# Decay exponents from spare rows of a TensorE product, two-part operands for y_diag and dt, and shortened norm chains, in a two-layer trunk

## The chip, the cores and the metric

The kernel runs on one core of one Trainium2 chip. The metric is the device time of one execution in microseconds (us), and lower is better. Engines are named as in the profile: PE is TensorE (the matrix engine), PEld its loading of the stationary operand, DVE VectorE, ACT ScalarE, POOL GpSimd, SP SyncE, which issues the DMAs.

## The reference

Input x holds 512 tokens of 1024 features in float32. Layer 0 runs Mamba-2 (SSD) heads and forgetting attention behind one projection; layer 1 is a causal convolution module. Each layer is `x + RMSNorm_post(mixer(RMSNorm_pre(x)))`. The part that matters most here is the SSD, with 16 heads of 64 features in 4 groups, 4 chunks of 128 tokens and a state of 128:

```python
xd = x * dt;  da = dt * a;  cs = cumsum(da over the 128 tokens of a chunk)
seg = cs[l] - cs[s]                                    # l query, s key, one head
decay = exp(where(l >= s, seg, -inf))
cb = einsum('bclgn,bcsgn->bclsg', cc, bc)              # one per group and chunk
y_diag = einsum(cb * decay, xd)
chunk_states = einsum(bc, xd * exp(cs[-1] - cs));  h = h * exp(cs[-1]) + state
y_off = einsum(cc, h_in) * exp(cs)
y = rmsnorm_by_group((y_diag + y_off + xs * d_skip) * silu(z_ssd)) * ssd_norm
o = softmax(q k / 8 + c_t - c_s, causal) v * silu(z_fox)     # c = cumsum(log forget gate)
x = x + rmsnorm(concat(y, o) @ w_out, g_post)
```

## The kernel before

Every product is done in float32r with each operand split into a high and a low part: `hi` is a cast, `lo` a subtraction, and a product is three matmuls, hi·hi, hi·lo and lo·hi (`mm3`, three calls of `mm` at line 102, so that all matmuls of the profile have that line, and are told apart by their tiles).

The weights are cut into 138 jobs of 0.5 MB, each worked off in 8 chunks of three matmuls of 512 columns (or six of 256): jobs 0 to 55 are the in-projection of layer 0 (xbc, z_ssd, z_fox, v, q and k), 56 to 71 its output projection, 72 to 121 the in-projection of layer 1, 122 to 137 its output projection. In the code `JO` is 56, `J1` 72 and `JO1` 122. `out_proj` computes the first half of the columns in jobs 56 to 63 (`first`) and the second in 64 to 71 (`second`), and `finish(b)` does the norm of one block of 128 tokens when its last product is there.

TensorE runs in the order in which the code is written. A planner, `Steps`, puts the steps of the SSD and of attention between the chunks of the jobs: a step may start when its needs are done and a delay has passed, counted in estimated TensorE microseconds (`now`, raised by each matmul). The delays of the SSD are the twelve numbers `DL`; `DL[11]` is that between the scaling by the gated norm (`gs`) and the transposes `yT`. The other engines are ordered by a scheduler, in which `high_priority` moves work ahead, and each of them works through its queue in order.

The steps of one SSD group: `silus` and `bc_parts` make B and C and their parts; `x_tokens` transposes x and scales it by dt (`xd`, split into parts); `cbT` makes the product cb and copies it out; `seg(h)` makes the decay exponents of a head: a matmul (`bc`) whose stationary operand is a column of `sel2`, broadcast, spreads cs[l] to all 128 partitions, then four DVE operations, one per chunk, add −cs[s] (`tk`) and a mask of 0 or a large negative number (`maskT`), and ACT takes the exponent. `mprod(h)` multiplies by cb and splits; `ydiag(h)` does three matmuls of 64 columns per chunk; `states` and `state_parts` make the running state H and its parts (`hll` is a low part); `yoff` the inter-chunk part `yo`; `gate` adds yd into y and multiplies by silu(z); `gate_sums` and `gate_scale` are the group's norm.

For 52 of the later weight tiles the low part is prepared beforehand. This early stream (`lo_ahead`) loads a weight tile (`pre`, line 202), casts it on ACT (`prh`, line 211), subtracts on DVE (line 212) and stores the low part to DRAM (`lo`, line 216). `run` calls it once per so many chunks, as the diff shows.

`rstd_of` (line 346 its DVE operation, 348 the power on POOL) and `scaled` (364, 367) are the norms; line 106 is the transposes. `dt` is a product of 48 columns (`dtf`), done together with the first three jobs in two halves of 256 tokens.

Of the kernel before, what the change touches and what calls it, by code (L numbers as in the profile page):

```python
# [12 lines left out]
ALU = mybir.AluOpType  # L13
# [23 lines left out]
def trunk(  # L37
# [306 lines left out]
    def rstd_of(ss, n):  # L344
        v = col("var", ss.shape[-1])
        V.tensor_scalar(v, ss, 1.0 / n, EPS, ALU.mult, ALU.add)  # L346
# [10 lines left out]

    def scaled(dst, xs):

        s2 = col("s2", 2)  # L360
        for i, t in enumerate(xs):
            sumsq(t, s2[:, i : i + 1])
        if len(xs) == 2:
            V.tensor_tensor(s2[:, 0:1], s2[:, 0:1], s2[:, 1:2], ALU.add)
        r = rstd_of(s2[:, 0:1], D)
# [59 lines left out]
    G.memset(maskT, 0.0)  # L425
    G.affine_select(out=maskT, in_=maskT, compare_op=ALU.is_ge, fill=NEG, base=0,
# [205 lines left out]
    def out_proj(w, stages, nk, gpost, resid, done, hooks):  # L632
# [27 lines left out]
        def first(k2, wh, wl):  # L660
# [46 lines left out]
        def finish(b):  # L707
            ss = sumsq(pb1[b])
            y1 = [o0[b], t2("y1")]
            V.tensor_tensor(y1[1], pb1[b], gpost[1], ALU.mult)  # L710
            V.tensor_tensor(ss, ss, s0[b], ALU.add)
            r = rstd_of(ss, D)
# [392 lines left out]
    dh, dl = t2("dh", F32R)[:, : KT * 48], t2("dl", F32R)[:, : KT * 48]  # L1105
    wdt = [lambda k, t=t: t[:, k * 48 : (k + 1) * 48] for t in (dh, dl)]
# [15 lines left out]
    split(dh, dl, raw[:, : KT * 48], A.copy, V)  # L1122
# [69 lines left out]
    chl = cp.tile([80, 2, S], F32R, name="chl")  # L1192
# [3 lines left out]
    V.tensor_scalar(chl[64:80], f32(chl)[32:48], -1.0, None, ALU.mult)  # L1196

# [404 lines left out]
```

## Time and profile before

| what | value |
|---|---|
| time, median of 3 runs | 939.8 us (937.92 to 940.81) |
| profiled execution | 940.86 us |
| its span, first to last instruction | 939.1 us |
| granted TensorE clock, mean | 0.993 of full |
| PE busy | 906.6 us (97%) |
| DVE busy | 731.1 us (78%) |
| ACT busy | 605.3 us (64%) |
| POOL busy | 511.6 us (54%) |
| data moved | 166.14 MB, 177 GB/s over the span |

In a row of the profile, `out<-in` are the tiles written and read, then come partitions × elements and the count; "busy" is the time with at least one such instruction at work, and the "mean" is that of one from its start to its modelled end, so that the means of pipelined matmuls overlap. In a timeline each line begins with the start and the duration, and the bracket tells how long the engine stood idle before and what it waited for. In a table of windows the columns are the length, then the busy time (and count) of PE, PEld, DVE, ACT and POOL, the granted clock, the DMA share and GB/s.

### The profile page before, as it was taken

The page shows a single profiled execution, that of the slowest core. Times are in us where ns is not written, and L with a number is a line of the kernel's source. Part 1 is how long each engine was busy: PE and PEld are TensorE (multiplying, and loading weights), DVE is VectorE, ACT ScalarE, POOL GpSimd, SP SyncE. Part 2 cuts the span into 40 slices and gives each one's busy share as a digit, 9 for nine tenths or more (in the row PEclk, how much of TensorE's full clock was granted, in tenths as well). Part 3 has the DMA queues.
Part 4 walks back from the last instruction along what each step waited for, and adds up shares of the span by engine and source line. Part 5 has one row for each costly group of instructions (what it writes and reads, how often), then busy time and mean ns, then how long its engine had stood idle before and what let it go on. Part 6 is the DMA issues. An engine that isn't in the chain of part 4 may idle for free.

```text
span 939.1 us, 13909 instructions
## 1 busy us (share of the span) xinstructions
PE 906.6 (97%) x4683; PEld 755.6 (80%) x4683; DVE 731.1 (78%) x1284; ACT 605.3 (64%) x1134; POOL 511.6 (54%) x476
## 2 busy tenths in 40 slices
PE   6999999998999999989899989999999999999997
PEld 6887787787798888778678879888888887787885
DVE  5667968788977887988877347899999999979502
ACT  5757667576855767677575536987886877658300
POOL 2604554535633444445573111998999999847310
PEclk9999999999999999999999999999999999999999
DMA  7725631347765574674538986546564665554503
GB/s 208 229 77 180 202 90 53 104 128 237 241 202 159 163 243 158 182 244 150 168 110 285 333 301 227 169 157 213 180 209 150 190 197 174 157 157 155 182 1 112
DMA packets 182507, 166.14 MB, mean 177 GB/s; under 512 B 7900, under 2 KB 151908, under 8 KB 182436
## 3 DMA queue, kind: packets, MB, share of 16 engines
q1 hardware_dynamic: 182420, 165.25, 54.9%
q8 instruction: 37, 0.61, 0.3%
q14 instruction: 34, 0.28, 0.1%
q10 hardware_dynamic: 16, 0.00, 0.0%
HBM read 133.64 MB, written 31.46 MB: 176 GB/s over the span
## 4 chain that ended last, share of the span: by engine, by line
PE 42%; DVE 6%; DMA 5%; issue 2%; ACT 2%; SPq 1%; POOL 1%; DVEq 0%; POOLq 0%; ACTq 0%
PE m L102 29%; PE o L102 10%; DMA lo<-pre 3%; DVE pre L212 2%; DMA wr<-in_o_w_in_dram 1%; PE acc L102 1%; PE tm L102 1%; DMA wr<-in_e_w_out_dram 1%; DVE w L191 1%; PE s L102 1%; DVE pl L119 1%; PE pT L106 0%; DMA pre<-in_o_w_in_dram 0%; ACT pr L95 0%; DMA pre<-in_o_w_out_dram 0%
## 5 line engine op out<-in xcount | busy, mean ns | idle before, releaser
L102 PE MATMUL m<-uh,w 128*128 128x512 f32 (+1 forms) x1392 | 453.5, 393 | 0.0
L102 PEld LDWEIGHTS m<-uh,w 128*128 128x128 f32 x1392 | 261.4, 190 | 50.9 <-issue 3.1
L102 PE MATMUL m<-ul,w 128*128 128x512 f32 (+1 forms) x696 | 267.7, 385 | 0.0
L191 POOL TENSOR_TENSOR w<-wr,w 128x512 fp32r<-128x512 f32 x112 | 158.8, 1442 | 160.3 <-ACT w L159 123.6
L984 DVE SCALAR_TENSOR_TENSOR acc<-h,cw,acc 128x490 f32<-128x490 f32 (+13 forms) x274 | 179.0, 731 | 2.7 <-ACT acc L976 2.0
L891 POOL TENSOR_TENSOR acc<-acc,prod 128x507 f32<-128x507 f32 (+9 forms) x124 | 159.6, 1289 | 8.2 <-ACT prod L877 0.7
L102 PEld LDWEIGHTS m<-ul,w 128*128 128x128 f32 x696 | 132.3, 190 | 21.5 <-issue 0.5
L102 PE MATMUL o<-w,hlh 128*128 128x512 f32 x448 | 142.2, 399 | 2.3 <-ACT pr L95 2.3
L212 DVE TENSOR_TENSOR pre<-pre,prh 128x512 fp32r<-128x512 f32 x104 | 90.6, 889 | 44.8 <-ACT prh L211 44.6
L102 PEld LDWEIGHTS o<-w,hlh 128*128 128x128 f32 x448 | 83.4, 191 | 19.0 <-ACT pr L95 3.0
L102 PE MATMUL tm<-w,uh 128*128 128x256 f32 (+1 forms) x384 | 91.7, 330 | 1.9 <-ACT pr L95 0.9
L211 ACT CAST prh<-pre 128x512 fp32r<-128x512 f32 x104 | 61.2, 622 | 48.5 <-DMA pre<-in_o_w_in_dram 14.6
L1464 POOL TENSOR_SCALAR pr<-pr,ri 128x128 f32<-128x128 f32 (+1 forms) x64 | 39.7, 621 | 92.6 <-DVE ri L1463 85.8
L159 ACT CAST w<-wr 128x1024 fp32r<-128x1024 f32 x72 | 74.8, 1048 | 23.0 <-DMA wr<-in_e_w_in_dram 6.6
L102 PE MATMUL o<-w,hll 128*128 128x512 f32 x224 | 88.0, 393 | 0.0
L877 ACT ACTIVATE prod<-h,cw 128x507 f32<-128x507 f32 (+9 forms) x124 | 79.0, 709 | 0.0
L348 POOL TENSOR_TENSOR rstd<-var,mhalf 128x1 f32<-128x1 f32 (+1 forms) x20 | 14.0, 698 | 114.6 <-DVE var L346 114.6
L157 ACT CAST w<-wr 128x1024 fp32r<-128x1024 f32 x56 | 57.2, 1050 | 18.5 <-DMA wr<-in_o_w_out_dram 10.3
L102 PEld LDWEIGHTS tm<-w,uh 128*128 128x128 f32 x384 | 62.9, 190 | 7.6 <-DVE QS L605 1.1
L102 PE MATMUL tm<-w,ul 128*128 128x256 f32 (+1 forms) x192 | 61.2, 319 | 0.0
L95 ACT ACTIVATE pr<-s,nmx 128x128 f32<-128x128 f32 (+1 forms) x64 | 34.0, 531 | 38.0 <-DVE nmx L1458 27.8
L102 PEld LDWEIGHTS o<-w,hll 128*128 128x128 f32 x224 | 42.6, 190 | 9.0
(270 smaller groups left out, 1594.3 us busy)
## 6 DMA issues: line engine op xcount, KB each, us to landing
wr<-in_e_w_in_dram SPq DMA_DIRECT2D x56, 512.0 KB
lo<-pre SPq DMA_DIRECT2D x52, 512.0 KB
pre<-in_o_w_in_dram SPq DMA_DIRECT2D x48, 512.0 KB
wr<-in_o_w_in_dram SPq DMA_DIRECT2D x48, 512.0 KB
w<-lo SPq DMA_DIRECT2D x48, 512.0 KB
wr<-in_e_w_out_dram SPq DMA_DIRECT2D x16, 512.0 KB
wr<-in_o_w_out_dram SPq DMA_DIRECT2D x16, 512.0 KB
x<-in_x_dram SPq DMA_DIRECT2D x12, 256.0 KB
```

What stands on the lines that cost most here:

```text
L95: i = A.activation(*a, **kw)
L102: T.matmul(o, l, r, start=start, stop=stop, skip_group_check=True)
L157: last_cast[0] = A.copy(hi, src).ins
L159: last_cast[0] = A.copy(hi, src).ins
L191: j.eng.tensor_tensor(hl[1][i][:, sl], src[:, sl], f32(hl[0][i])[:, sl], ALU.subtract)
L211: A.copy(h[:, sl], t[:, sl])
L212: V.tensor_tensor(t.bitcast(F32R)[:, sl], t[:, sl], f32(h)[:, sl], ALU.subtract)
L348: mark["rstd"] = G.tensor_tensor(r, v, mhalf.to_broadcast([P, ss.shape[-1]]), ALU.pow).ins
L877: A.activation(prs[i][:, s:], hs[j][:, : S - s], AF.Copy, scale=w31(30 - s, j))
L891: G.tensor_tensor(a2[j][:, s:], a2[j][:, s:], prs.pop(i)[:, s:], ALU.add)
L984: V.scalar_tensor_tensor(a[:, s:], h[:, : S - s], w31(30 - s, j), a[:, s:], ALU.mult, ALU.add)
L1464: G.tensor_scalar(p[:, :L], p[:, :L], ri, 1.0, ALU.mult, ALU.mult)
```

## The change

Parts, in the order of the diff:

1. The early stream runs at one call per 7 chunks up to job 69, where it ran at one per 11 from job 56 on.
2. The norm chains: the first half's sum of squares is already scaled and given EPS by `part_var`, and `rstd_of` takes it in with the second half's. `finish` calls `rstd_of` before the product with `gpost`.
3. `z_ssd`, `v_proj` and the first job of layer 0's `out_proj` loop over token blocks outside and weight rows inside.
4. dt: the high and low part of its weights stand in one operand of 112 columns, so that two matmuls per row tile do the three products; the result's two pieces are added by one more DVE operation.
5. Exponents: the stationary operand of `bc` is a tile `sel` of 128 rows, made once per group: rows 0 to 47 choose cs of the head, and rows 64 to 71 hold cs of the keys in hi and lo for the four chunks (16 small DMAs from `chl`), against indicator rows in `cs2`. The matmul so gives cs[l] − cs[s], and one DVE operation bounds it at 88. The mask holds 1 and 0, and is multiplied into cb as it is copied out, on DVE.
6. `ydiag`: `xd` tiles hold hi and lo of a head side by side, and hi of the decay product is multiplied with both at once (128 columns), lo with hi (64 columns). `yadd` adds the pieces into y for each pair of heads, four operations; `gate` only multiplies.
7. `states` and `state_parts` get high priority on DVE and ACT; `DL[11]` goes from 6 to 9.

```diff
-                if 5 <= i < 13 or 26 <= i:
-                    if (8 * i + c) % (11 if i >= JO else 7 if i >= 26 else 8) == 0:
+                if 5 <= i < 13 or 26 <= i < J1 - 2:
+                    if (8 * i + c) % (7 if i >= 26 else 8) == 0:
                         next(early, None)
...
+    def rstd_of(ss, n, pre=None):
+            V.scalar_tensor_tensor(v, ss, 1.0 / n, pre, ALU.mult, ALU.add)
+    def part_var(ss, n):
+        p = col("pre")
+        V.tensor_scalar(p, ss, 1.0 / n, EPS, ALU.mult, ALU.add)
...
-            for j in range(2):
-                k = 2 * k2 + j
-                for b in range(NB):
+            for b in range(NB):
+                for j in range(2):
+                    k = 2 * k2 + j
...
         def finish(b):
             ss = sumsq(pb1[b])
+            r = rstd_of(ss, D, s0[b])
             y1 = [o0[b], t2("y1")]
             V.tensor_tensor(y1[1], pb1[b], gpost[1], ALU.mult)
-            V.tensor_tensor(ss, ss, s0[b], ALU.add)
-            r = rstd_of(ss, D)
...
+    def dt_chunks(sl):
+        for k in range(KT):
+            w = dhl[k // 4][:, k % 4 * P : k % 4 * P + 112]
+            mm(first[0][:112, sl], w, uh[k][:, sl], k == 0, False)
+            mm(first[0][:48, sl], w[:, :48], ul[k][:, sl], False, k == KT - 1)
...
+    cs2 = cp.tile([P, S], F32R, name="cs2")
+    V.tensor_tensor(cs2[64:72, :].rearrange("p (c l) -> p c l", c=4), i4[0], i4[1], ALU.add)
-    DL = [2, 7, 4, 11, 4, 9, 4, 9, 9, 3, 3, 6]
+    DL = [2, 7, 4, 11, 4, 9, 4, 9, 9, 3, 3, 9]
...
+        sel = st["sel"] = t2("sel", F32R)
+        G.memset(f32(sel), 0.0)
+        A.copy(h4(sel[:48, :]), f32(sel2)[:48, 4 * g : 4 * g + 4].unsqueeze(2).to_broadcast([48, 4, P]))
+        for h in range(4):
+            r = 96 + 4 * g + h
+            nc.sync.dma_start(f32(sel)[64:72, h * P : h * P + P], f32(chl)[r : r + 1, :, :])
...
-            A.copy(st["cb"], cb)
+            V.tensor_tensor(st["cb"]..., cb..., maskT.unsqueeze(1).to_broadcast([P, 4, P]), ALU.mult)
...
-        mm(bc, sel2[:, h : h + 1].to_broadcast([48, P]), cs2, True, True)
+        mm(bc, SG[h // 4]["sel"][:, h % 4 * P : h % 4 * P + P], cs2, True, True)
-        for c in range(NB):
-            V.scalar_tensor_tensor(s[:, tok(c)], bc[:, tok(c)], tk[:, c, 32 + h : 33 + h], maskT, ALU.add, ALU.add)
+            V.tensor_scalar(s, bc, 88.0, None, ALU.min)
...
-            mm3(o, mh[:, tok(c)], ml[:, tok(c)], xh, xl, True, True)
+            mm(o, mh[:, tok(c)], x, True, False)
+            mm(o[:, :64], ml[:, tok(c)], x[:, :64], False, True)
+    def yadd(g, pair):
+            for i in range(2):
+                for t in range(2):
+                    V.tensor_tensor(ys, ys, parts[:, :, :, t, :], ALU.add)
     def gate(g):
-                V.tensor_tensor(y[i], y[i], yd[i], ALU.add)
```

How it moves the instructions, at three places. On DVE at the end of layer 0, where the norm of the second block of tokens is finished (`y` is the product with `gpost`, `ss` and `var` the norm's sums, `pre` the early stream's subtraction, `u` the input of layer 1), before:

```order
L710 TENSOR_TENSOR y_1329_6195<-o_1258_5902,x_5662 128x512 [waits Activation_49]
L711 TENSOR_TENSOR ss_6192<-ss_6192,ss_5881 128x1
L212 TENSOR_TENSOR pre_6102<-pre_6102,prh_6247 128x512 [waits DMAHW7_49,DMAHW4_49,Activation_49]
L346 TENSOR_SCALAR var_6198<-ss_6192 128x1 [waits DVE_49]
L212 TENSOR_TENSOR pre_6102<-pre_6102,prh_6247 128x512 [waits Activation_49]
L714 SCALAR_TENSOR_TENSOR o_1248_5880<-o_1248_5880,rstd_6200,x_6070 128x512 [waits Pool_49]
```

and after:

```order
L349 SCALAR_TENSOR_TENSOR var_6182<-ss_6179,pre_5875 128x1 [waits DVE_49,Activation_49]
L717 TENSOR_TENSOR y_1362_6186<-o_1294_5908,x_5642 128x512
L719 SCALAR_TENSOR_TENSOR o_1278_5871<-o_1278_5871,rstd_6184,x_6074 128x512 [waits DMAHW7_49,Pool_49]
L719 SCALAR_TENSOR_TENSOR y_1362_6186<-y_1362_6186,rstd_6184,x_6075 128x512 [waits DMAHW0_49,DVE_49]
L364 TENSOR_SCALAR pre_6199<-ss_6196 128x1 [waits Activation_49]
```

The two subtractions of the early stream are gone from between the norm's operations (they stand ahead of the first block's norm now), and `var` comes before the product. (The `pre` of L364 is the norm's column, not the stream's tile.)

On PE in the first SSD group, where the exponents of its first heads stand among the z_ssd product `tm`, before:

```order
L102 MATMUL bc_960<-cs_564,sel_565 128x512 [waits DVE_49,PE_49]
L102 MATMUL tm_786<-w_793,uh_143 128x512
L102 MATMUL tm_786<-w_793,uh_143 128x512 [waits Pool_49]
L102 MATMUL tm_786<-w_793,ul_151 128x512
L102 MATMUL bc_971<-cs_564,sel_565 128x512 [waits DVE_49,PE_49]
```

and after:

```order
L102 MATMUL bc_969<-cs_561,sel_820 128x512 [waits DVE_49,DMAHW4_49,PE_49,Activation_49]
L102 MATMUL tm_786<-w_791,uh_140 128x512 x2
L102 MATMUL tm_786<-w_791,ul_148 128x512
L102 MATMUL bc_977<-cs_561,sel_820 128x512 [waits DMAHW5_49,DVE_49,PE_49]
L102 MATMUL tm_786<-w_791,uh_141 128x512 x2
```

The order of `bc` and `tm` is much the same; `bc` now waits for one of the DMAs that fill `sel`, and `tm` stays with a block of tokens (tm_786) where the block changed.

On SP at the same group (`wr` are weights of the jobs, `pre` and `lo` the early stream's load and store), before:

```order
L216 DMA lo_851<-pre_707 128x1024 [waits DMAHW2_49,DVE_49]
L163 DMA wr_1094<-in_e_w_in_dram 128x8x128 [waits DMAHW7_49,Activation_49,Pool_49]
L202 DMA pre_853<-in_o_w_in_dram 128x8x128 [waits DMAHW2_49]
L216 DMA lo_928<-pre_744 128x1024 [waits DMAHW5_49,DVE_49]
L202 DMA pre_930<-in_o_w_in_dram 128x8x128 [waits DMAHW6_49,DMAHW5_49]
```

and after:

```order
L216 DMA lo_856<-pre_705 128x1024 [waits DMAHW2_49,DVE_49]
L163 DMA wr_1091<-in_e_w_in_dram 128x8x128 [waits DMAHW7_49,Activation_49,Pool_49]
L1287 DMA sel_820<-chl 8x1x128 [waits Pool_49]
L1287 DMA sel_820<-chl 8x1x128 [waits DMAHW5_49]
L1287 DMA sel_820<-chl 8x1x128 [waits DMAHW6_49]
L1287 DMA sel_820<-chl 8x1x128
L202 DMA pre_858<-in_o_w_in_dram 128x8x128 [waits DMAHW2_49,DMAHW0_49]
```

The four small DMAs stand behind a weight load and ahead of the early stream's next load, and the first of them waits for POOL, which clears `sel`.

More of the change, by code (lines that the diff above doesn't have):

```diff
@@ L356, in sumsq @@
         return ss
+    def part_var(ss, n):
+        p = col("pre")
+        V.tensor_scalar(p, ss, 1.0 / n, EPS, ALU.mult, ALU.add)
+        return p
     def scaled(dst, xs):
[L360 to L365, printed above, removed]
+        pre = part_var(sumsq(xs[0]), D)
+        r = rstd_of(sumsq(xs[1]), D, pre)
         for t, u in zip(xs, dst):
@@ L424, in trunk @@
     maskT = cp.tile([P, P], F32, name="maskT")
-    G.memset(maskT, 0.0)
-    G.affine_select(out=maskT, in_=maskT, compare_op=ALU.is_ge, fill=NEG, base=0,
+    G.memset(maskT, 1.0)
+    G.affine_select(out=maskT, in_=maskT, compare_op=ALU.is_ge, fill=0.0, base=0,
                     pattern=[[1, P]], channel_multiplier=-1)
@@ L664, in first @@
                     lead_in()
-            for j in range(2):
-                k = 2 * k2 + j
-                for b in range(NB):
+            stagger = k2 == 0 and len(stages) == 1
+            for j, b in ((j, b) for b in range(NB) for j in range(2)) if stagger else ((j, b) for j in range(2) for b in range(NB)):
+                    k = 2 * k2 + j
                     step(pb0[b], b, k, wh(j), wl(j))
@@ L1121, in trunk @@
     to_uT(uh, ul, 0, us[0:2], c0, True)
-    split(dh, dl, raw[:, : KT * 48], A.copy, V)
+    dt_parts()
     for b in range(2, 4):
@@ L1126, in trunk @@
             split_to(b)
-    ws = [wdt] + [jobs[i].w for i in range(3)]
+    ws = [None] + [jobs[i].w for i in range(3)]
     def together(js, half):
-        gens = [fm_chunks(first[i], P if i else 48, *ws[i], uh, ul, slice(half * 256, half * 256 + 256)) for i in js]
+        sl = slice(half * 256, half * 256 + 256)
+        gens = [fm_chunks(first[i], P, *ws[i], uh, ul, sl) if i else dt_chunks(sl) for i in js]
         for _ in zip(*gens):
@@ L1202, in trunk @@
     V.tensor_copy(cs2[32:48, :], f32(csl)[0:16, :])
-    V.tensor_tensor(sel2, ident[0:48, 0:16], ident[0:48, 32:48], ALU.add)
+    i4 = [ident[64:72, 64 + 4 * i : 68 + 4 * i].unsqueeze(2).to_broadcast([8, 4, P]) for i in range(2)]
+    V.tensor_tensor(cs2[64:72, :].rearrange("p (c l) -> p c l", c=4), i4[0], i4[1], ALU.add)
+    V.tensor_tensor(sel2, ident[:, 0:16], ident[:, 32:48], ALU.add)
     tk = cp.tile([P, NB, P], F32, name="tk")
@@ L1266, in x_tokens @@
         with tc.high_priority(offset=HP):
-            st.setdefault("xd", []).append(hilo(pb))
+            xd = [t2("xd", F32R) for _ in range(2)]
+            src = pb.rearrange("p (c h f) -> p c h f", c=2, h=4)
+            parts = [t.rearrange("p (h t f) -> p h t f", h=4, t=2) for t in xd]
+            for c, t in enumerate(parts):
+                A.copy(t[:, :, 0, :], src[:, c])
+            for c, t in enumerate(parts):
+                V.tensor_tensor(t[:, :, 1, :], src[:, c], f32(t[:, :, 0, :]), ALU.subtract)
+            st.setdefault("xd", []).extend(xd)
             a = t2("xe")
@@ L1318, in state_parts @@
         r = []
-        for i, w in enumerate((512, 256)):
-            r.append(hilo(H[i][:, :w], w))
+        with tc.high_priority(offset=HP):
+            for i, w in enumerate((512, 256)):
+                r.append(hilo(H[i][:, :w], w))
         SG[g]["H"] = [p[0] for p in r], [p[1] for p in r]
```

73 lines of the change are left out of this document (47 added, 26 removed).

## The prediction, made before the changed kernel ran

> **What bounds the kernel.** I read the page's busy shares first, then the granted clock, then what TensorE waits for, and then the timeline and 20 us windows at the places that the diff touches.
>
> ```profile
> PE 906.6 (97%) x4683; PEld 755.6 (80%) x4683; DVE 731.1 (78%) x1284; ACT 605.3 (64%) x1134; POOL 511.6 (54%) x476
> core 0: 939.1 us, clock 0.993
> ```
>
> TensorE works in 906.6 of 939.1 us, so the time is its work plus 32.5 us of gaps. What ends these gaps is listed by the waits of TensorE (out, line, releaser: total us, times, longest):
>
> ```profile
> PE uT L106 <- DVE x L367: 6.1, 3, 3.7
> PE uT L106 <- DVE u L367: 2.8, 1, 2.8
> PE yT L106 <- DVE y L1388: 2.6, 2, 1.6
> PE o L102 <- ACT pr L95: 2.5, 4, 0.9
> PE yo L102 <- DVE hll L119: 2.0, 2, 1.6
> PE s L102 <- ACT pr L95: 1.5, 2, 0.8
> PE tm L102 <- DVE QS L605: 0.9, 1, 0.9
> ```
>
> They are few and short, and each stands at one place. So there are two ways to gain: fewer TensorE microseconds (one for one where TensorE is full), and these places. The other engines count only where they hold TensorE.
>
> **1. y_diag: 192 matmuls become 128.** A head is 12 matmuls of 64 columns before; after, it is 4 of 128 columns and 4 of 64. Start times on TensorE, one head of group 0, then cb (128 columns), and the group row:
>
> ```profile
> 100.10 0.19 PE L102 MATMUL yd<-hlh,hlh 128*128 128x64 f32 x1
> 100.13 0.28 PE L102 MATMUL yd<-hll,hlh 128*128 128x64 f32 x1
> ...
> 101.24 0.28 PE L102 MATMUL yd<-hlh,hll 128*128 128x64 f32 x1
> 101.35 0.48 PE L102 MATMUL m<-uh,w 128*128 128x512 f32 x1
> 178.27 0.27 PE L102 MATMUL cb<-hlh,hll 128*128 128x128 f32 x1
> ...
> 179.28 0.27 PE L102 MATMUL cb<-hlh,hll 128*128 128x128 f32 x1
> L102 PE MATMUL yd<-hlh,hll 128*128 128x64 f32 x64 | 17.7, 277 | 0.0
> ```
>
> Busy times of pipelined matmuls overlap, so I price by the distance of starts. From the second of the twelve yd to the last are ten steps, (101.24 − 100.13)/10 = 0.111 us each. The cb rows, twice as wide, stand at (179.28 − 178.27)/9 = 0.112. The ends are 0 (two old matmuls' columns cost as much in one) and this; I take this, as the cb rows are of just that width: width up to 128 costs nothing, and 16 heads × 4 matmuls saved × 0.111 give **−7.1 us**. A rule of the Trainium skill speaks against it: "TensorE: Matmul & The Clock Gate", section "Back-to-back issue gap", lists for isolated matmuls some 60 cycles up to 64 columns and 134 cycles at 128. By it, as an estimate, 192 × 25 ns = 4.8 us would become 64 × 56 + 64 × 25 ns = 5.2 us, and the edit would bring nothing. The same section says that pairs of weight load and matmul are spaced wider than that; the trace, where 64 and 128 columns cost the same, decides for the sum, and the rule stays as a rival.
>
> **2. The seg row product.** One 512-column matmul per head with 48 rows of contraction becomes one with 128 rows.
>
> ```profile
> 85.25 0.40 PE L102 MATMUL tm<-w,ul 128*128 128x512 f32 x1
> 85.58 0.49 PE L102 MATMUL bc<-cs,sel 48*128 48x512 f32 x1
> ...
> 86.57 0.39 PE L102 MATMUL tm<-w,ul 128*128 128x512 f32 x1
> ...
> 87.27 0.39 PE L102 MATMUL tm<-w,ul 128*128 128x512 f32 x1
> ```
>
> From one tm<-w,ul to the next are two more tm: 87.27 − 86.57 = 0.70 us without a bc between, 86.57 − 85.25 = 1.32 us with one. So a bc costs 0.62 to 0.63 us, against 0.23 (0.70/3) for a 512-column matmul of 128 rows; the gap stands on both sides of it. With 128 rows I take the normal 0.23: 16 × 0.40 = **−6.4 us**. Bounds: 0 if the gap is not due to the 48 rows, −6.4 if it all is; a loss is excluded, since the new product has the shape of the tm beside it. I take the full gain for that same reason.
>
> The stationary operand now waits for more: a POOL memset, an ACT cast and four SP DMAs per group, which stand in SP's queue behind a weight load and ahead of the next transfers. In groups 1 to 3 POOL's place is behind a weight split that the next weight load needs anyway, so I cost that at nothing. In group 0 the bound is 0 to 2 us of TensorE wait; it goes into the sundries below.
>
> **3. DVE work of the SSD stage.** Prices (a 512-column, a 256-column, and the old exponent row):
>
> ```profile
> L1347 DVE SCALAR_TENSOR_TENSOR seg<-bc,tk,maskT 128x128 f32<-128x128 f32 x64 | 17.7, 343 | 3.1 <-PE bc L102 3.0
> L1372 DVE TENSOR_TENSOR y<-y,yd 128x512 f32<-128x512 f32 x8 | 5.2, 680 | 0.0
> 213.47 0.42 DVE L1333 TENSOR_TENSOR yo<-yo,tk 128x256 f32<-128x256 f32 x1
> 100.00:120.00 20.00, 17.96 (x107) 15.51 (x106) 19.49 (x24) 10.57 (x22) 11.37 (x8) 1.00 0.54 159
> ```
>
> seg: 64 operations, 17.7 us, become 16 of 512 columns at 5.2/8 = 0.65: −7.3. The y adds: 8 × 0.65 become 32 × 0.42: +8.2. Four masked cb evacuations come from ACT: +2.6. The x·dt tiles, 8 subtractions of 512 columns to 16 of 256: +1.5. Sum +5 us of DVE over some 200 us of SSD work, where DVE mostly has slack. In group 0 it has none (last row: 19.49 of 20.00 busy), and the yo wait of 2.0 us there, behind hll, is left at **0** (−2 if the state chain's new priority removes it, +2 if the adds lengthen it). The adds are not on TensorE's path elsewhere: the yd banks come free one pair earlier than before.
>
> **4. dt projection: 48 matmuls become 32.**
>
> ```profile
> 28.49 0.28 PE L102 MATMUL dtf<-uh,dl 128*48 128x256 f32 x1
> 28.61 0.28 PE L102 MATMUL m<-uh,w 128*128 128x256 f32 x1
> ```
>
> 0.12 us each. In the first half of the tokens TensorE waits for x and the first weights anyway, so only the second half's 8 count: **−0.9 us**. The extra DVE operation and the tile memsets hide behind the same waits.
>
> **5. The end of layer 0.** From DVE's, then TensorE's timeline, and the window (PE, PEld, DVE, ACT, POOL, clock, DMA share, GB/s):
>
> ```profile
> 552.16 0.15 DVE L711 TENSOR_TENSOR ss<-ss,ss 128x1 f32<-128x1 f32 x1
> 557.05 0.69 DVE L212 TENSOR_TENSOR pre<-pre,prh 128x512 fp32r<-128x512 f32 x1 [4.75 <-ACT prh L211]
> 557.66 0.15 DVE L346 TENSOR_SCALAR var<-ss 128x1 f32<-128x1 f32 x1
> 562.67 2.29 PE L106 MATMUL uT<-ident,u 128*128 128x128 f32 x14 [2.81 <-DVE u L367]
> 560.00:580.00 20.00, 17.33 (x125) 16.68 (x126) 13.00 (x34) 10.79 (x28) 2.76 (x5) 0.91 0.95 331
> ```
>
> The norm's var stood in DVE's queue behind a subtraction of the early weight stream, which waited 4.75 us for its load; TensorE then stood 2.81 us, and the granted clock fell: 0.91 over 20 us is (1 − 0.91) × 20 = 1.8 us more. The new order has no such operation there, since the stream ends before job 67, and the chain is shorter by an add. 4.75 is more than 2.81, so the whole goes: **−4.6 us**. Late next is the rstd on POOL and u itself, which then run under the last products.
>
> **6. The yT wait of one group.**
>
> ```profile
> 212.86 0.69 DVE L212 TENSOR_TENSOR pre<-pre,prh 128x512 fp32r<-128x512 f32 x1 [4.44 <-ACT prh L211]
> 222.99 0.76 PE L106 MATMUL yT<-ident,y 128*128 128x128 f32 x3 [1.61 <-DVE y L1388]
> 220.00:240.00 20.00, 17.44 (x78) 13.78 (x77) 17.17 (x26) 15.06 (x25) 13.72 (x10) 0.91 0.81 258
> ```
>
> Here too a late subtraction held the chain (yo, gate, rstd, y), with 2.6 us of wait and 1.8 of clock, 4.4 in all. DL[11] from 6 to 9 puts 15 more matmuls ahead of yT, 75 for 60: 15 × 0.23 = 3.5 us, more than 2.6, and the yd adds leave the gate. I take three quarters, **−3.3 us** (0 to −4.4), because the stream's load may come late again.
>
> **7. Tail and attention.**
>
> ```profile
> 933.03 0.69 DVE L710 TENSOR_TENSOR y<-o,x 128x512 f32<-128x512 f32 x1 [3.75 <-ACT junk L355]
> ...
> 933.82 0.15 DVE L346 TENSOR_SCALAR var<-ss 128x1 f32<-128x1 f32 x1
> 455.25 0.73 PE L102 MATMUL o<-w,hlh 128*128 128x512 f32 x2 [0.67 <-ACT pr L95]
> 440.00:460.00 20.00, 17.21 (x85) 13.08 (x84) 17.97 (x33) 12.76 (x28) 10.52 (x13) 0.95 0.74 246
> ```
>
> At the very end var now runs first and y moves under POOL's rstd: 933.82 − 933.03 = **−0.75 us**. The loops with token block outside change which bank is freed and filled when; around attention 2.5 + 1.5 + 0.9 of wait and 0.05 × 20 = 1.0 of clock stand, 5.9 in all, behind ACT's exponentials, which the change does not touch. I take **−2.5** (0 to −5.9), as other matmuls move between.
>
> **8. Sundries.** The stream now splits 13 tiles in jobs 56 to 66 instead of 8, and there is the sel chain of group 0: **+1.5 us** (0 to +10, see the third rival).
>
> ```profile
> 480.00:500.00 20.00, 19.65 (x103) 15.91 (x102) 15.51 (x24) 15.87 (x29) 11.75 (x12) 1.00 0.46 142
> 520.00:540.00 20.00, 20.00 (x90) 16.54 (x90) 5.40 (x8) 8.97 (x17) 2.54 (x2) 1.00 0.98 331
> ```
>
> **Sum:** −7.1 − 6.4 − 0.9 − 4.6 − 3.3 − 0.75 − 2.5 + 1.5 = −24.05. The profiled execution took 940.86 us (its span 939.1 and 1.76 around it), 1.1 above the median of 939.8; 940.86 − 24.05 = 916.8, and half the distance to the median off gives 916.3, rounded to **916**.
>
> **Rivals.** What a measurement can tell from no change here is about 0.3%, 2.8 us.
> - *DVE takes the SSD gain back.* Where DVE is full, a shorter TensorE only waits longer. For it: group 0, and +5 us of DVE. Against it: TensorE is at 17.4 to 20 of 20 us elsewhere. Price: a quarter of items 1 and 2 (3.4), half of the rest (5), and item 6 lost (3.3), some 11 us after rounding: **927**.
> - *Width counts for yd,* so that 128 columns cost as much as two matmuls of 64: item 1 falls, 916 + 7 = **923**. The cb rows speak against it. (It is the case that the rule of item 1 gives.) Likewise, *bc doesn't get cheaper* (the gap belongs to the change of operand, not to the 48 rows): 916 + 6.4 = **922**.
> - *Slower: the early stream starves the weights.* Jobs 56 to 66 lie at about 474 to 534 us (24 products of 0.23 a job, 5.5 us, counted back from the uT at 562.67, where job 71 ends). There five more tiles of 0.5 MB in and 0.5 MB out are 5 MB, 15 us of transfer at the 331 GB/s of the second row above, where the share is 0.98 already; a cast or subtraction that waits 4.4 to 4.75 us for its load holds ACT and DVE, and behind them the evacuations of out_proj. Each costs TensorE up to 4.6; five give back 23, and from six on the kernel is slower: 916 + 27.6 = **944**. Against it: the first row has room (0.46), weights are loaded ahead, and four of the five tiles are taken from just behind, where the share is as high.
> - *More goes:* all of the attention waits and the yo wait vanish too, 916 − 3.4 − 2 − 1.5 = **909**.
>
> **Chances.** The forecast (911 to 921) 0.55; DVE takes it back 0.21; width counts 0.03; bc stays dear 0.05; more goes 0.08; slower 0.05; a mix of the first and the third rival that ends within 2.8 us of before 0.03. So faster 0.92, same 0.03, slower 0.05. The range of 907 to 929 takes in the forecast and the first, second and fourth rivals with 2 us around them, and leaves out some 1 in 10.
>
> **What would show it.** The profile after should have yd rows of 128 and 64 columns at a distance of 0.11 us, a bc among tm at 0.23 and not 0.63, no wait of uT at the end of layer 0 and a clock near 1.00 there, yT waits under 1 us, a PE busy time some 15 to 18 us lower (the products, and the matmuls that ran at the low clock), and about 27 us of gaps. It is wrong if seg or yo waits on DVE appear in each group, if tm or o in jobs 56 to 71 wait for a weight, or if bc waits for the sel DMAs.

## The result, and the profile after

| | before | changed |
|---|---|---|
| median of 6 runs | 939.8 us (937.92 to 940.81) | 934.5 us (931.02 to 937.22) |
| ratio, 95% interval | | 0.9939 (0.9916 to 0.9963) |
| profiled execution | 940.86 | 931.02 |
| its span | 939.1 | 929.3 |

The change is worth 5.3 us (3.5 to 7.9 by the interval), and 24 were forecast. The profiled execution of the changed kernel is the fastest of its six, so between the two profiles there are 9.8 us; what the other five lost was not profiled.

The page's busy line, the granted clock, and the longest waits of TensorE after:

```profile
PE 895.6 (96%) x4603; PEld 751.0 (81%) x4603; DVE 746.6 (80%) x1276; ACT 605.7 (65%) x1144; POOL 516.1 (56%) x482
core 0: 929.3 us, clock 0.988
PE uT L106 <- DVE x L372: 5.6, 2, 4.8
PE yT L106 <- DVE y L1443: 4.5, 4, 1.9
...
PE xt L106 <- ACT cv L95: 2.2, 1, 2.2
...
PE yd L102 <- DVE hll L119: 1.4, 1, 1.4
PE tm L102 <- DVE QS L611: 1.0, 1, 1.0
```

The uT wait on `u` at the end of layer 0 is gone (the one on `x` is the kernel's start, 6.1 us before). The yT wait grew from 2.6 to 4.5 us, xt and yd are new, and the mean clock fell from 0.993 to 0.988. The products themselves became as cheap as priced. TensorE's timeline after, one head of yd and one bc:

```profile
97.73 0.22 PE L102 MATMUL yd<-xd,hlh 128*128 128x128 f32 x1
...
98.53 0.48 PE L102 MATMUL m<-uh,w 128*128 128x512 f32 x1
...
242.19 0.39 PE L102 MATMUL bc<-cs,sel 128*128 128x512 f32 x1
242.43 0.39 PE L102 MATMUL m<-uh,w 128*128 128x512 f32 x1
```

A head takes 98.53 − 97.73 = 0.80 us for its eight yd, where twelve took 1.25; a bc takes 242.43 − 242.19 = 0.24 us, where it took 0.63. So 13 to 14 us of TensorE work did go. What came in its place stands in two windows (columns as before: length, PE, PEld, DVE, ACT, POOL, clock, DMA share, GB/s):

```profile
100.00:120.00 20.00, 18.59 (x82) 15.79 (x82) 19.27 (x29) 8.82 (x18) 8.05 (x7) 0.83 0.36 107
220.00:240.00 20.00, 13.28 (x47) 9.98 (x46) 17.51 (x20) 13.24 (x26) 14.20 (x12) 0.66 0.64 189
```

By the clock the first lost (1 − 0.83) × 20 = 3.4 us. In the second, 0.66 means 13.6 us at half speed, but TensorE stood idle for 3.0 of them (the last yT wait and the xt wait below), which a full clock would not have shortened; so the clock took (13.6 − 3.0)/2 = 5.3 us there. Beside that, 1.4 and 6.7 us of gaps stand in the two windows. GpSimd, VectorE and TensorE in the second:

```profile
219.46 1.01 POOL L351 TENSOR_TENSOR rstd<-var,mhalf 128x4 f32<-128x4 f32 x1 [5.49 <-DVE var L347]
220.44 2.54 POOL L191 TENSOR_TENSOR w<-wr,w 128x512 fp32r<-128x512 f32 x2
222.95 1.31 POOL L119 TENSOR_TENSOR hll<-cv,hlh 128x512 fp32r<-128x512 f32 x1
...
220.50 5.17 DVE L1443 TENSOR_SCALAR y<-y,rstd 128x256 f32<-128x256 f32 x4 [0.41 <-POOL rstd L351]
...
222.00 0.30 PE L106 MATMUL yT<-ident,y 128*128 128x128 f32 x1 [1.89 <-DVE y L1443]
223.19 0.33 PE L106 MATMUL yT<-ident,y 128*128 128x128 f32 x1 [0.89 <-DVE y L1443]
224.46 0.47 PE L106 MATMUL yT<-ident,y 128*128 128x128 f32 x1 [0.94 <-DVE y L1443]
225.73 0.48 PE L106 MATMUL yT<-ident,y 128*128 128x128 f32 x1 [0.80 <-DVE y L1443]
...
232.03 0.90 PE L106 MATMUL xt<-ident,cv 128*128 128x128 f32 x3 [2.20 <-ACT cv L95]
```

TensorE is at the transposes of the third group's y before the norm is. The norm's four short scale operations on VectorE take 5.17 us together, and the transposes behind them start 1.2 to 1.3 us apart, which is the length of one GpSimd operation (2.54/2). Then xt waits as well, and from 225.7 to 238 us matmuls stand at 0.43 us instead of 0.23.

### The profile page after: what moved, and what is told of

Its sections match the earlier page's. It is cut to its first block, busy times and chain, and to the rows that moved or that the text cites. A ratio compares the mean times of both kernels' runs of the same rounds, so it can differ in the third digit from the quotient of the medians.

```text
span 929.3 us, 13844 instructions
## 1 busy us (share of the span) xinstructions
PE 895.6 (96%) x4603; PEld 751.0 (81%) x4603; DVE 746.6 (80%) x1276; ACT 605.7 (65%) x1144; POOL 516.1 (56%) x482
## 4 chain that ended last, share of the span: by engine, by line
PE 53%; DVE 5%; DMA 2%; issue 1%; ACT 1%; POOL 0%; DVEq 0%; POOLq 0%; ACTq 0%
PE m L102 31%; PE o L102 18%; PE tm L102 1%; DVE pre L212 1%; PE s L102 1%; DMA pre<-in_o_w_in_dram 1%; PE pT L106 1%; PE acc L102 1%; DMA lo<-pre 1%; DVE pl L119 1%; DVE nmx L1515 0%; DVE w L191 0%; PE uT L106 0%; DVE os L1548 0%; DVE KX L624 0%
## 5 line engine op out<-in xcount | busy, mean ns | idle before, releaser
L191 POOL TENSOR_TENSOR w<-wr,w 128x512 fp32r<-128x512 f32 x112 | 161.9, 1470 | 162.6 <-ACT w L159 104.2
L102 PEld LDWEIGHTS m<-ul,w 128*128 128x128 f32 x696 | 133.1, 191 | 21.7 <-issue 0.5
L102 PE MATMUL o<-w,hlh 128*128 128x512 f32 x448 | 140.2, 394 | 0.8 <-ACT pr L95 0.8
L212 DVE TENSOR_TENSOR pre<-pre,prh 128x512 fp32r<-128x512 f32 x104 | 94.3, 924 | 27.7 <-ACT prh L211 27.5
L159 ACT CAST w<-wr 128x1024 fp32r<-128x1024 f32 x72 | 75.0, 1049 | 18.3 <-DMA wr<-in_e_w_in_dram 7.3
L211 ACT CAST prh<-pre 128x512 fp32r<-128x512 f32 x104 | 60.9, 620 | 39.8 <-DVE pre L212 17.7
```

What stands on the lines that cost most here:

```text
L102: T.matmul(o, l, r, start=start, stop=stop, skip_group_check=True)
L159: last_cast[0] = A.copy(hi, src).ins
L191: j.eng.tensor_tensor(hl[1][i][:, sl], src[:, sl], f32(hl[0][i])[:, sl], ALU.subtract)
L211: A.copy(h[:, sl], t[:, sl])
L212: V.tensor_tensor(t.bitcast(F32R)[:, sl], t[:, sl], f32(h)[:, sl], ALU.subtract)
```

## Experiments

Each was timed in 5 rounds beside the kernel before; ratios are to that, so 0.9939 is "as the changed kernel". To see where a kernel gains and loses, I counted the matmuls of the weight jobs along TensorE's timeline weighted by their columns, and compared the time at which the same share of them was done, in the profiled execution. Around jobs 30 and 38 the SSD's steps stand at other places among the jobs in each kernel, and a lead can swing by some us within 20 us; jobs 62 and 80 lie in steadier stretches. The changed kernel's profiled execution is 3.5 us faster than its median, so its row looks better by as much than its ratio. Negative is ahead of the kernel before:

```
                    ratio  (95%)            job 30  job 38  job 62  job 80
                                            (235)   (292)   (502)   (609 us)
changed             0.9939 (0.9916-0.9963)   -8.7    -4.4    -4.0    -8.9
scale_on_act        0.9856 (0.9837-0.9876)  -18.5   -10.7    -7.6   -12.5
yt_later            0.9973 (0.9956-0.9991)   -8.1    -3.7    +2.1    -2.1
yd_later            0.9903 (0.9890-0.9916)  -13.3    -9.9    -3.9    -8.5
early_old           0.9965 (0.9948-0.9982)   -9.4    -5.2    -5.8    -6.0
bc_alone            0.9985 (0.9972-0.9998)   -0.1    -1.7    -1.0    -2.1
yd_alone            0.9990 (0.9973-1.0008)   -1.1    -1.0    -0.9    -1.0
half_adds           0.9935 (0.9923-0.9948)  -12.2    -9.0    -3.2    -7.7
act_and_later       0.9891 (0.9876-0.9905)  -17.1   -11.1    -6.6   -10.9
stream_late         0.9918 (0.9896-0.9939)  -16.1   -18.6   -18.3    -7.5
act_stream_late     0.9918 (0.9894-0.9943)  -19.2   -21.7   -20.5    -7.7
before_stream_late  1.0071 (1.0045-1.0097)   -3.1    -3.0    -0.8    +9.7
loops_old           0.9932 (0.9910-0.9954)  -11.2    -7.9    -0.6    -5.3
stream_out          0.9907 (0.9886-0.9928)   -8.9   -11.4   -11.0    -9.6
before_stream_out   1.0027 (1.0006-1.0048)   -2.0    -2.0    -2.4    +2.7
bc_stream_out       0.9982 (0.9968-0.9996)   -5.6    -7.2    -8.4    -4.6
yd_stream_out       1.0036 (1.0021-1.0051)   -2.4    -2.1    -1.7    +1.4
stream_fit          0.9805 (0.9784-0.9826)  -12.7   -15.2   -12.8   -16.6
stream_fit_act      0.9843 (0.9821-0.9864)  -13.8   -14.6    -8.4   -12.0
```

### The stalls one by one

**scale_on_act**

```diff
-                V.tensor_scalar(q256(y, c), q256(y, c), r[:, c : c + 1], None, ALU.mult)
+                A.activation(q256(y, c), q256(y, c), AF.Copy, scale=r[:, c : c + 1])
```

> The changed kernel, with the four multiplications by rstd of gate_scale on ScalarE instead of VectorE; TensorE's order is the same. Theory A: in the profile after, the yT of the third group waits 1.9 + 0.9 + 0.9 + 0.8 us because each of the four short VectorE operations takes 1.27 us beside GpSimd's weight subtractions, and the 12 us at half clock and the 2.2 us wait of xt follow from it. Then the four waits shrink to one of under 1 us, the clock in 220 to 240 us stays near 1, and the time falls by 6 to 11 us against the changed kernel's 934.5. Theory B: the norm chain comes late in VectorE's queue anyway (5 us more work), and the scale operations only show it: the yT wait stays at 2 us or more and the time changes by less than 2 us.

926.9 us, 0.83% below the changed kernel. The sixteen operations in both kernels (shortest, median, longest in ns), then from scale_on_act the window, the wait that came, and where the third group's rstd starts:

```profile
L1443 DVE TENSOR_SCALAR y<-y,rstd x16: 338/1134/1382, 118.8 to 280.8; 128x256 f32<-128x256 f32 x16
L1443 ACT ACTIVATE y<-y,rstd x16: 492/495/512, 118.0 to 277.0; 128x256 f32<-128x256 f32 x16
220.00:240.00 20.00, 17.19 (x83) 13.11 (x84) 13.31 (x21) 12.94 (x23) 12.24 (x9) 1.00 0.71 225
276.32 0.73 PE L106 MATMUL yT<-ident,y 128*128 128x128 f32 x2 [2.42 <-ACT y L1443]
212.34 1.01 POOL L351 TENSOR_TENSOR rstd<-var,mhalf 128x4 f32<-128x4 f32 x1 [7.13 <-DVE var L347]
```

The stall went as theory A said: yT does not wait there, the clock stays whole, and the kernel is 18.5 us ahead at job 30. But that the length of the four operations had held it is not shown by this run. The edit also changed the order of the other work on VectorE and ScalarE, and the third group's rstd, which comes before any scale operation, starts at 212.34 us, 7.1 us earlier than in the changed kernel (219.46). At job 38 the kernel is 10.7 us ahead and at job 62 only 7.6. The fourth group's yT (the row of 276.32) and attention's first steps wait instead.

**yt_later** and **yd_later**

```diff
-    DL = [2, 7, 4, 11, 4, 9, 4, 9, 9, 3, 3, 9]
+    DL = [2, 7, 4, 11, 4, 9, 4, 9, 9, 3, 3, 16]     # yt_later
+    DL = [2, 7, 4, 11, 4, 9, 4, 14, 9, 3, 3, 9]     # yd_later
```

> The changed kernel with DL[11] at 16 instead of 9: some 30 more matmuls of the jobs, 7 us, stand ahead of each group's yT. Both theories say that the yT waits of the third group go (5.7 us from the first to the last transpose are covered); if the half clock and the xt wait that follow are their consequence, the time falls by 6 to 11 us. If they have causes of their own (too little work in the array, VectorE behind), it falls by 2 to 5 us at most, and the wait turns up at xt or at another step.

> The changed kernel with DL[7] at 14 instead of 9: each yd stands later behind its decay product. Theory C: in the first group the shorter bc and yd let TensorE run ahead of VectorE, which is the bound there; the 1.4 us wait of yd and the 7 us at half clock behind it go, and the time falls by 3 to 5 us, with the third group's yT wait unchanged. Rival: VectorE is so far behind that the wait returns at yo or yT of the first group, and the time is the same within 2 us.

yt_later came out 0.34% slower than the changed kernel (the two intervals just overlap), which neither theory had. The yT waits did go, and others came (TensorE's timeline of yt_later):

```profile
164.34 0.55 PE L106 MATMUL xt<-ident,cv 128*128 128x128 f32 x3 [3.77 <-ACT cv L95]
...
243.99 0.47 PE L102 MATMUL m<-uh,w 128*128 128x512 f32 x1 [2.96 <-DVE y L1314]
...
293.11 0.45 PE L102 MATMUL s<-KS,QS 128*128 128x128 f32 x1 [2.93 <-DVE KS L625]
```

yd_later gained 0.36% as theory C said, and the wait of yd in the first group is gone. By place the lead does not last: 9.9 us at job 38 and 3.9 at job 62, where the changed kernel has 4.4 and 4.0, with waits at xt (2.2), yo (2.1) and yT (2.3). **act_and_later** (both edits) tells the same:

> The changed kernel with the multiplication by rstd on ScalarE and DL[7] at 14. If the two waits, of yT in the third group and of yd in the first, are separate, the gains of the two single edits add: 0.8% and 0.4%, ratio 0.982 against the kernel before. If the waits only move on to the next step that VectorE or ScalarE holds, the sum stays at the better one's 0.986 or above.

It came out at 0.9891, no better than the scale edit alone (0.9856). So the waits move: a step that TensorE reaches next is late too.

**half_adds**

```diff
-                for t in range(2):
-                    V.tensor_tensor(ys, ys, parts[:, :, :, t, :], ALU.add)
+                V.tensor_tensor(ys, ys, parts[:, :, :, 0, :], ALU.add)
```

> The changed kernel, leaving out the add of the second piece of each y_diag product (xd's low part times the high part): 16 VectorE operations fewer, some 6 to 7 us of its time, nothing else. Theory D with VectorE as the one that is late: the waits of the first and third group shrink and the time falls by 3 to 8 us against 934.5. If VectorE's amount of work is not the matter, but only where GpSimd's operations fall beside it, the time moves by less than 3 us, in either direction.

No change in the time (0.9935); by place it is 4.6 us ahead of the changed kernel at job 38, and no longer at job 62. VectorE's amount of work is not what holds in the end, which also speaks against my first rival in the form in which I had put it.

### The parts alone

**bc_alone** is the kernel before with part 5 of the change, **yd_alone** the kernel before with part 6:

```diff
-        mm(bc, sel2[:, h : h + 1].to_broadcast([48, P]), cs2, True, True)          # bc_alone
+        mm(bc, SG[h // 4]["sel"][:, h % 4 * P : h % 4 * P + P], cs2, True, True)
...
-            mm3(o, mh[:, tok(c)], ml[:, tok(c)], xh, xl, True, True)               # yd_alone
+            mm(o, mh[:, tok(c)], x, True, False)
+            mm(o[:, :64], ml[:, tok(c)], x[:, :64], False, True)
```

> The kernel before with the exponents' part alone: sel tiles with the keys' exponents in rows 64 to 71, one VectorE operation per head, the mask in cb. The products by themselves: 16 bc at 0.23 instead of 0.63 us, 6.4 us less on TensorE. Theory D (the products are cheaper as priced, and the gain is lost in waits when the SSD runs ahead of VectorE, GpSimd and ScalarE): at job 38 the kernel is 3 to 6 us ahead of the one before, with waits at other steps. Theory E (the gain passes whole): 6 to 7 us faster, ratio 0.993.

> The kernel before with y_diag's part alone: products of 128 and 64 columns, the adds per pair of heads, interleaved xd tiles. TensorE does 7.1 us less, VectorE 9 to 10 us more. Theory D: the waits of yo, yT and xt grow, and the time changes by 0 to -4 us. Theory E: 7 us faster, ratio 0.9925.

They gave 0.15% and 0.10% (the second with an interval that takes in no change), where the products are worth 0.68% and 0.75%. Theory D had the direction; bc_alone's lead at job 38 is 1.7 us, where 3 to 6 were expected. What ate bc's gain stands in one place (ScalarE, VectorE, TensorE of bc_alone):

```profile
210.27 1.15 ACT L211 CAST prh<-pre 128x512 fp32r<-128x512 f32 x2 [5.18 <-DMA pre<-in_o_w_in_dram]
210.92 0.69 DVE L212 TENSOR_TENSOR pre<-pre,prh 128x512 fp32r<-128x512 f32 x1 [5.57 <-ACT prh L211]
221.06 0.66 PE L106 MATMUL yT<-ident,y 128*128 128x128 f32 x2 [4.73 <-DVE y L1400]
```

A tile of the early weight stream comes late from DRAM; ScalarE and VectorE, each in order, stand 5 us for it, with yo, the gate and the norm of the third group queued behind. TensorE is at the transposes at 216.3 us (221.06 − 4.73), where it was at 221.4 before (222.99 − 1.61), and waits 3.1 us longer. The group's end hangs on the stream, not on TensorE's work. In the kernel before the same wait was 4.44 us (the row 212.86 in the prediction). In yd_alone it is a yd of the third group (VectorE, then TensorE):

```profile
200.16 1.74 DVE L212 TENSOR_TENSOR pre<-pre,prh 128x512 fp32r<-128x512 f32 x1
201.82 0.41 DVE L1383 TENSOR_TENSOR y<-y,yd 128x256 f32<-128x256 f32 x1
202.16 0.41 DVE L1321 TENSOR_TENSOR H<-H,st 128x256 f32<-128x256 f32 x1
202.71 0.45 PE L102 MATMUL yd<-xd,hlh 128*128 128x128 f32 x1 [4.43 <-DVE H L1321]
```

It waits for an add of the running state H, which stands in VectorE's queue behind a subtraction of the stream that takes 1.74 us there; the matmuls behind it stand at 0.43 us, at half speed.

### The early stream

**stream_late** and, on the kernel before, **before_stream_late**:

```diff
-                if 5 <= i < 13 or 26 <= i < J1 - 2:
-                    if (8 * i + c) % (7 if i >= 26 else 8) == 0:
+                if 5 <= i < 13 or 34 <= i < J1 - 2:
+                    if (8 * i + c) % (6 if i >= 26 else 8) == 0:
```

> The changed kernel with the early stream's second stretch in jobs 34 to 69 at one call per 6 chunks instead of 26 to 69 at one per 7: no tile of it is loaded, cast or subtracted between about 195 and 265 us. Theory F: the third group's norm chain is late because VectorE and ScalarE, each in order, wait for the stream's loads (2 to 5.6 us around 205 to 211 us) with the chain behind; then the yT waits (4.5 us), the xt wait (2.2) and the 12 us at half clock behind them go, and the time falls by 7 to 11 us against 934.5, ratio 0.983 to 0.987. Theory A alone (GpSimd's subtractions beside the four scale operations): the waits stay, and the time moves by under 3 us. More transfers later may cost some us at the end of layer 0.

> The kernel before with only the early stream moved as in stream_late. By theory F the third group's yT wait (2.6 us and 1.8 of clock) goes, and with the stream's end before job 70 the uT wait (2.8 and 1.8) as well: 7 to 9 us faster, ratio 0.991. By the rival, that the SSD is held by VectorE's amount of work, only the second goes: 4 to 5 us.

**act_stream_late** has the scale edit too:

> The changed kernel with the scale operations on ScalarE and the early stream moved as in stream_late. If A and F hold the same waits, it is no faster than the better of the two (ratio 0.986); if each holds its own, it comes to 0.980 or below, near the 916 us that I had forecast (0.975).

In time all three missed. By place, theory F held for the changed kernel: 18.6 us ahead at job 38 and 18.3 at job 62, near the 17.7 of my terms for dt, yd, bc and yT together (0.9 + 7.1 + 6.4 + 3.3); the kernel before is 3.0 ahead at job 38 by the same move. With the stream away, the scale edit brings 2 to 3 us more by place (21.7 and 20.5) and nothing in the time. Then most of the lead is paid back at the end of layer 0. Windows of the third group, its scale operations, then VectorE and TensorE at the end of layer 0, in stream_late:

```profile
200.00:220.00 20.00, 20.00 (x98) 16.75 (x98) 18.05 (x25) 10.76 (x22) 11.73 (x10) 1.00 0.33 96
220.00:240.00 20.00, 20.00 (x115) 17.27 (x114) 13.81 (x25) 17.30 (x31) 7.94 (x7) 1.00 0.31 90
211.24 5.28 DVE L1443 TENSOR_SCALAR y<-y,rstd 128x256 f32<-128x256 f32 x4 [0.41 <-POOL rstd L351]
...
544.75 0.75 DVE L719 SCALAR_TENSOR_TENSOR y<-y,rstd,x 128x512 f32<-128x512 f32 x1 [5.13 <-DMA x<-in_x_dram]
...
548.11 0.69 PE L106 MATMUL uT<-ident,u 128*128 128x128 f32 x2 [5.71 <-DVE u L372]
554.07 2.18 PE L106 MATMUL uT<-ident,u 128*128 128x128 f32 x9 [5.28 <-DVE u L372]
```

The four scale operations are as long here as in the changed kernel (5.28 us), but they start 9.3 us earlier, and no yT waits: what the stream holds is the norm's arrival, and the length of these operations costs only where the norm is late. At the end, the stream makes its last call two to three jobs later, its last loads stand ahead of the residual loads of x, and the norm waits for x.

**stream_out** and **before_stream_out** have the stream in jobs 5 to 23 (one call per 11 chunks) and 34 to 69 (one per 7); **bc_stream_out** and **yd_stream_out** are bc_alone and yd_alone with that stream.

```diff
-                if 5 <= i < 13 or 26 <= i < J1 - 2:
-                    if (8 * i + c) % (7 if i >= 26 else 8) == 0:
+                if 5 <= i < 24 or 34 <= i < J1 - 2:
+                    if (8 * i + c) % (7 if i >= 26 else 11) == 0:
```

> The changed kernel with the early stream's 55 calls in jobs 5 to 23 (one per 11 chunks) and 34 to 69 (one per 7): out of the third and fourth group, as in stream_late, but at the end of layer 0 at the pace of the changed kernel. Theory F: the SSD stage keeps the 20 us that stream_late had at job 62, the uT waits of 5 us do not come, and the time is 914 to 922 us (ratio 0.972 to 0.98), where my forecast was. Rival: the stream's work only moves its harm into the first and second group (waits of yd, yo or xt between 110 and 200 us); then 928 us or more.

> The kernel before with only the same move of the stream. The yT wait of the third group (2.6 us, 1.8 of clock) and the uT wait (2.8 and 1.8) go: 7 to 9 us faster, ratio 0.991, with the products as before. If it stays at 0.996 or above, the stream costs the kernel before little, and only the changed products meet it.

> bc_alone with the stream so moved. Theory F: now the 6.4 us of the products pass whole: 5.5 to 7.5 us faster than before_stream_out. If VectorE's work holds the SSD, they pass in part, 2 to 4 us.

> yd_alone with the stream so moved. Theory F: 6 to 8 us faster than before_stream_out. If VectorE's 10 us more work holds the SSD, 0 to 3 us.

The rival had it: the harm moved into the second group, and the stream, in whose count I had been off, ended three jobs later than the changed kernel's. before_stream_out did not gain either (1.0027, expected 0.991): it has a uT wait of 5.3 us at the end of layer 0 and a yo wait of 2.7. TensorE of stream_out:

```profile
161.63 0.42 PE L102 MATMUL yd<-xd,hll 128*128 128x64 f32 x1 [2.55 <-DVE hll L119]
...
553.02 2.23 PE L106 MATMUL uT<-ident,u 128*128 128x128 f32 x14 [3.85 <-DVE u L372]
```

Against before_stream_out, bc passed almost whole by place, 6.0 us at job 62 (−8.4 to −2.4), and 4.2 us in the time (0.9982 to 1.0027), below the 5.5 to 7.5 expected. yd passed not at all (1.0036), with waits of yd in the second group, where the stream is.

**stream_fit** puts it in jobs 5 to 16 (one per 8) and from 34 on (one per 6), ending where the changed kernel's ends; **stream_fit_act** has the scale edit and starts at job 32.

```diff
+                if 5 <= i < 17 or 34 <= i < J1 - 2:
+                    if (8 * i + c) % (6 if i >= 26 else 8) == 0:
```

> The changed kernel with the early stream in jobs 5 to 16 (one call per 8 chunks) and from 34 on (one per 6): no tile of it in the third and fourth group, few in the second, and its last loads ahead of the residual loads of x at the end of layer 0, as in the changed kernel. Theory F: 18 to 20 us ahead of the kernel before at job 62, no uT wait over 2 us, and 915 to 922 us (ratio 0.974 to 0.981). Rival: the queues are so full between 500 and 550 us that a TensorE that comes 15 us earlier waits for the residual loads whatever the stream's order; then the uT wait is 4 us or more and the time 926 us or more.

> The same with the scale operations on ScalarE and the stream from job 32 on, so that it ends two jobs earlier. If the end of layer 0 is bound by the residual loads behind the stream, its uT wait is smaller than in stream_fit by 1 to 4 us; if not, the two are alike within 2 us.

stream_fit took 922.9 us, ratio 0.9805 (0.9784 to 0.9826): 1.3% below the changed kernel and the fastest of all that ran, though 1 to 8 us slower than expected. It is 15.2 us ahead at job 38, with waits of 1.7 us at yT and 1.3 at xt in the first and second group, and at the end of layer 0 it has no uT wait:

```profile
220.00:240.00 20.00, 20.00 (x105) 16.73 (x104) 13.24 (x23) 15.10 (x26) 10.39 (x9) 1.00 0.38 109
540.00:560.00 20.00, 20.00 (x131) 18.22 (x130) 12.09 (x30) 8.21 (x23) 2.75 (x5) 1.00 0.83 294
```

stream_fit_act ended earlier still and has no uT wait either, but lost 6.2 us between jobs 38 and 62, where stream_fit lost 2.4. So a TensorE that comes earlier to the end of layer 0 does not wait for the residual loads as such; it did where the stream ended later.

### Two smaller terms

**early_old** is the changed kernel with the stream's old pace from job 56 on; **loops_old** has the old loop order in `z_ssd`, `v_proj` and `out_proj`.

```diff
-                if 5 <= i < 13 or 26 <= i < J1 - 2:                                # early_old
-                    if (8 * i + c) % (7 if i >= 26 else 8) == 0:
+                if 5 <= i < 13 or 26 <= i:
+                    if (8 * i + c) % (11 if i >= JO else 7 if i >= 26 else 8) == 0:
...
-            for b in range(NB):                                                    # loops_old
-                for j in range(2):
+            for j in range(2):
+                for b in range(NB):
```

> The changed kernel with the early stream's old pace (one call per 11 chunks from job 56 on, up to job 71). My term: the wait of uT at the end of layer 0 (2.8 us and 1.8 of clock) went because no subtraction of the stream stands in the norm there any more; then it returns and the time rises by 3 to 5 us. Rival: the shortened chain alone removed it; then the time stays within 1 us.

> The changed kernel with the weight rows outside and the token blocks inside again in z_ssd, v_proj and out_proj. My term for attention was -2.5 us by this order; then the time rises by 2 to 3 us. The profile after shows the same waits around 395 to 475 us as before (5 to 6 us), so the rival: no change beyond 1.5 us.

early_old is 2.4 us slower than the changed kernel by the two ratios, whose intervals overlap; in its profile a uT wait of 2.1 us on `u` is back, and between jobs 62 and 80 it gains 0.2 us, where the changed kernel gains 4.9. loops_old takes the same time as the changed kernel (0.9932, median 934.5 for both). Its profiled execution loses 7.3 us between jobs 38 and 62, where the changed kernel's, its fastest, loses 0.4; with equal medians that is no effect of the loops.

## Why the prediction was wrong

- **y_diag, bc and dt (items 1, 2, 4)** were right as prices of TensorE work: 0.80 for 1.25 us a head, 0.24 for 0.63 us a bc, and 0.8 us at job 6. The rivals "width counts" and "bc stays dear" are out. Wrong was the sentence that a microsecond less is one for one where TensorE is full. In the third group TensorE was full because the next step happened to be ready; bc_alone and yd_alone show that it isn't when TensorE comes earlier. TensorE's busy time fell by 11.0 us (906.6 to 895.6), where 15 to 18 were forecast, and its gaps grew to 33.7 us, where 27 were forecast.
- **The yT wait (item 6), −3.3.** This is the step that failed most. It became 4.5 us of yT, 2.2 of xt and 5.3 of clock, 12.0 in all, against 4.4 before: +7.6. I had given 15 more matmuls of distance (3.5 us) and forgotten that items 1, 2 and 4 bring TensorE there earlier, while the norm does not come earlier by that. By the traces yT stands even 33 weight matmuls later in TensorE's order than before (7.6 us at 0.23), and yet TensorE is there at 220.1 us, before at 221.4. At the same place of its work it was 7.6 + 1.3 = 8.9 us ahead, and rstd came only 1.5 us earlier (220.99 to 219.46). What kept the norm back is the early stream: stream_late moves nothing else, and there the scale operations start 9.3 us earlier and the stall is gone. The second half of the wait (0.89 + 0.94 + 0.80 us) is the length of the scale operations, 1.3 us each beside GpSimd's operations, where three of the four took 0.35 in the third group before; no run takes this part away alone.
- **Group 0 (item 3), 0.** It became yd 1.4 and 3.4 of clock for yo 2.0, +2.8. My first rival named the place and gave 927 for it (half of the rest in its price is 3.6 us and not 5, which moves it by about 1 us); its cause, VectorE's amount of work, isn't borne out: with 16 adds fewer the yd wait here is still 1.4 us (half_adds), and so it is in stream_late, which leaves the stream in jobs 5 to 12 as it was. What holds this step is not shown.
- **The end of layer 0 (item 5), −4.6**, was right: the lead grew from 4.0 us at job 62 to 8.9 at job 80.
- **Tail (item 7), −0.75**, was right. VectorE before, then after:

```profile
934.70 0.75 DVE L714 SCALAR_TENSOR_TENSOR o<-o,rstd,x 128x512 f32<-128x512 f32 x1 [0.72 <-POOL rstd L348]
```
```profile
924.06 0.16 DVE L349 SCALAR_TENSOR_TENSOR var<-ss,pre 128x1 f32<-128x1 f32 x1 [4.51 <-ACT junk L358]
...
924.94 0.75 DVE L719 SCALAR_TENSOR_TENSOR o<-o,rstd,x 128x512 f32<-128x512 f32 x1
```

  From the first operation after the last sum to `o` it is 0.88 us, where it was 934.70 − 933.03 = 1.67.
- **Attention (item 7), −2.5**, was wrong: loops_old shows no effect of the loop order. The gaps between 395 and 475 us did not shrink (6.7 us before, 7.5 after). The windows from 440 to 480 us lost 1.6 us of clock before and nothing after, but by place nothing came of it: the lead is 4.4 us at job 38 and 4.0 at job 62. These 0.4 us are also all that shows of the sundries (item 8, +1.5); no bc waits for its DMAs. With them the pieces add up to −0.8 − 7.1 − 6.4 + 7.6 + 2.8 + 0.4 − 4.9 − 0.8 = −9.2, where the two profiles differ by 9.8.
- **The slower rival** (the stream starves the end of layer 0) did not come in the changed kernel, but stream_late and before_stream_late show its mechanism at 11 us.

Left open: whether the stream harms the third group by its late loads or by its operations on VectorE and ScalarE, since every edit moved both, and moving the stream changed the order of other instructions too; what holds the first group; and what the five runs beside the profiled one lost.

## What to carry to other kernels

Shortening the work of a full engine gains only until the next step that another chain holds. For each step behind the shortened work, ask when it would be ready if the engine came that much earlier, and look above all for in-order queues in which a background stream of transfers stands ahead of the critical chain. When cheaper products bring nothing, move the background work first, with the products unchanged and changed, and compare positions along the run, not only the end. When an edit takes a stall away, look whether it also moved the chain that came before it.

## What the hardware showed that I had not expected

Short waits cost TensorE its clock, and not always. In the changed kernel a yd wait of 1.41 us was followed by half speed from 104.6 to 111.6 us:

```profile
103.20 0.30 PE L102 MATMUL yd<-xd,hll 128*128 128x64 f32 x1 [1.41 <-DVE hll L119]
...
105.03 0.63 PE L102 MATMUL m<-ul,w 128*128 128x512 f32 x1
```

The same wait in scale_on_act and stream_late (1.44 and 1.43 us) left the clock of that window at 1.00, and so did the yo wait of 1.60 us before. All half-speed stretches of the twenty traces, but for the one at each end, last 3.41 us or a multiple of it. Cut into stretches of this length, in step with the changes of the clock, the traces give: of 5008 stretches at full speed with under 1.15 us without a matmul at work, none was followed by half speed; of 72 with 1.15 to 1.9 us, 19 were; of 35 with more, all were. The 1.41 us lay whole in one stretch, the 1.44 and 1.43 us in two each; but the 1.60 us lay in one too, so in between something else decides as well. The Trainium skill, "TensorE: Matmul & The Clock Gate", section "What's actually happening", says that the clock is set by a free-running activity window of some 3.4 us. The stretches of 3.41 us, and a wait that counts or not by where it falls, agree with this; that a whole idle window is needed, as its table has it, does not agree with 1.41 us.

VectorE's short scale operations took from 338 to 1382 ns, those of the third group 1.3 us each beside GpSimd operations of 1.27 us, and on ScalarE 492 to 512 ns. The Trainium skill's "SBUF — State Buffer", section "SBUF: two separate sides", describes a port pair that VectorE and GpSimd take by turns for a whole instruction; the starts of yT at GpSimd's pace agree.
